# A two-layer hybrid attention trunk: another planned attention phase, and the first FFN weight splits pinned

## The chip, the core and the metric

The kernel runs on one core of one Trainium2 chip. The metric is the device time of one execution in microseconds (us), the median of several runs. TensorE (PE) multiplies, VectorE (DVE), ScalarE (ACT) and GpSimd (POOL) do the elementwise work, and SyncE (SP) issues most of the transfers.

## The reference

Two layers are computed on 512 tokens of width 1024. Each layer normalizes, projects to 3080 columns, runs four differential heads and eight forgetting heads, projects back, adds the residual, and runs a SwiGLU FFN of width 2816 between norms.

```python
for l in range(DEPTH):                       # DEPTH = 2
    proj = rms_norm(x, attn_pre_g[l]) @ w_in[l]
    qa, ka, va, qb, kb, vb, f_logit = split(proj)
    qa, ka = partial_rotary(qa, cos, sin), partial_rotary(ka, cos, sin)   # 16 of 64 columns of a head
    oa = rms_norm(diff_attention(qa, ka, va, lam), diff_sub_g[l]) * (1 - lam_init)   # softmax0 - lam * softmax1
    ob = forgetting_attention(qb, kb, vb, log_sigmoid(f_logit + forget_bias[l]))
    x = x + rms_norm(concat(oa, ob) @ w_out[l], attn_post_g[l])
    h = rms_norm(x, ffn_pre_g[l])
    x = x + rms_norm((silu(h @ w_gate[l]) * (h @ w_up[l])) @ w_down[l], ffn_post_g[l])
```

## The kernel before

**Arithmetic.** A float32 product is made from three matmuls in the reduced float format. Each operand is split into a high part (a cast on ScalarE, `hi`, names with h) and a low part (the difference on VectorE or GpSimd, `lo`, names with l); `hh`, `hl` and `lh` are summed in PSUM. So each weight chunk costs one DMA into a raw buffer (`wr`, two of them), one cast and one difference, and no matmul with the low part can run before the difference is done. Activations are kept transposed as `hT_h` and `hT_l`.

**The planned attention phase.** All instructions of a layer's attention are added to a `Plan` (L71) with an engine, an estimated duration, their dependencies, a key (lower is more urgent) and the buffers that they take and give. `Plan.run` (L98) simulates the engines, picks the most urgent ready operation of each, and issues it. Every issued instruction is passed to `keep_in_program_order`, which ties an instruction behind the one traced last on the same engine; so each engine executes the plan's order. The estimates are `dV`, `dA` and `dG` (L372 to L379) for VectorE, ScalarE and GpSimd. Softmax steps have keys by head and query block; the projections (`tile_chunk`, L670) and the output projection's first half (`o0_chunk`, L1090) are fillers with the key 1e6, run by TensorE whenever nothing more urgent is ready.

**The start of layer 0.** `start` (L397) loads `x` and the value weights, normalizes each of four token tiles, transposes them and computes the values `va` of the tiles, with the keys 500 and up, ahead of all fillers; warm-up matmuls on zeros (`WARM`, on `sinT`) fill TensorE's gaps. `tables` (L525) then computes the rotary tables: positions by eight DMAs on SP, the angles on VectorE, sine and cosine on ScalarE, out to DRAM and back into `cosT` and `sinT`. The rotation of k and q (`t1`, `pair`, `t2`, `t3` in `tile_chunk`) waits for them. Layer 1 has no such start: its norms and values come out of the end of the first FFN.

**The end of the phase.** After the plan, the last output matmuls run tile by tile. `o_norm(t)` is `post_norm` (L304) and then `pre_norm` (L279): squares on ScalarE, the reciprocal root on GpSimd, products on VectorE. `o_norm(3)` is at L1195. After it, L1263 asks for the first chunks of the FFN:

```python
(g0, g0_part), (u0, u0_part), (g1, g1_part) = gate(0), up(0), gate(f1)
g0_part(h0)                      # h0: tokens 0 to 255
pre_T(2, hs[2], f"f{l}", [0])    # transposes of token tile 2
```

`gate` and `up` call `proj_T` (L320), which calls `load_w` (L247): a DMA, a cast on ScalarE and a difference on VectorE. These are not pinned before the change; a list scheduler places them by its own estimate of when they are ready. The matmuls and transposes of this stretch are pinned (`pinned[0]` is true from L618 to L1281). The second up chunk, `up(f1)`, follows the first SwiGLU product (L1278). The other chunks of the FFN, from L1282 on, are not pinned.

Of the kernel before, what the change touches and what calls it, by code (L numbers as in the profile page):

```python
# [17 lines left out]
P = 128  # L18
# [17 lines left out]
TB = S // 16  # L36
VA_C, VA_T = 4, 1
# [7 lines left out]
C_ID, C_M, C_F, NKEEP, C_U = 0, 128, 640, 641, 641  # L45
# [16 lines left out]
class Op:  # L62
    def __init__(self, eng, dur, fn, deps, key, take, give, lat):
        self.eng, self.dur, self.fn, self.key, self.take, self.give, self.lat = eng, dur, fn, key, take, give, lat
        self.users, self.after, self.left, self.ready, self.end = [], [], 0, 0.0, None
        for d in deps:
            d.users.append(self)
            self.left += 1


class Plan:  # L71


    def __init__(self, slots, margin):
        self.free = {k: [0.0] * n for k, n in slots.items()}
        self.margin, self.ops, self.last, self.idle = margin, [], {}, None

    def add(self, eng, dur, fn, deps=(), key=0.0, take=(), give=(), lat=0.0, order="", ready=0.0):
        o = Op(eng, dur, fn, deps, key, take, give, lat)
# [18 lines left out]
    def run(self, pin, first):  # L98
        clock = dict.fromkeys("VAGQ", 0.0)
        clock["P"] = first  # L100
        cands = {e: [o for o in self.ops if o.eng == e and not o.left] for e in clock}
        todo = len(self.ops)
        while todo:
            best = None
            for e, c in cands.items():
                opts = []
                for o in c:
                    s = self.slots_at(o)
                    if s is not None:
                        r = max(s, o.ready)  # L110
                        opts.append((max(r, clock[e]), o.key, r, o))
# [12 lines left out]
            clock[o.eng] = start + o.dur  # L124
            o.end = start + o.dur + o.lat
# [34 lines left out]
def _constants():  # L160
# [6 lines left out]
    c[:, C_M + S - P:C_M + S] = np.where(r[None, :] > r[:, None], np.float32(-BIG), np.float32(0.0))  # L167
    expo = np.arange(0, ROT, 2, dtype=np.float32) / np.float32(ROT)
    inv_freq = (np.float32(1.0) / np.power(np.float32(500000.0), expo).astype(np.float32)).astype(np.float32)
    c[:, C_F] = inv_freq[r // 16]  # L170
    return c
# [3 lines left out]
def hymba_block(ctx, tc, x_d, pos_d, apre_d, win_d, fb_d, lq1_d, lk1_d, lq2_d, lk2_d, dsg_d, wout_d, apost_d,  # L175
# [64 lines left out]
    V.memset(sinT, 0.0)  # L240
    G.memset(cosT, 1.0)
# [5 lines left out]
    def load_w(src, shape, name, eng=None, dst=None, raw=None):  # L247
# [10 lines left out]
        A.copy(hi, raw)  # L258
        (eng or V).tensor_sub(lo, raw, hi.bitcast(F32))  # L259
# [87 lines left out]
    for l in range(DEPTH):  # L347
        win = win_d[l]
        with ExitStack() as actx:
# [12 lines left out]
            mixed_d = ap.tile([P, NDIFF, S], F32, name=f"mixd{l}", tag="v8", bufs=5)  # L362
            if l == 0:
                raw_v = ap.tile([P, NDIFF, S], F32, name=f"rawv{l}", tag="v8", bufs=5)
# [18 lines left out]
            vd, tab = [], []  # L383
# [12 lines left out]

            def start():  # L397

                plan.free.update(g=[], v8=[0.0], qs=[], ks=[])
# [9 lines left out]
                idd = dma(con[:, :P], con_d[:, :P], P)  # L409

                def w_load(c):
                    raw = (mixed_d, raw_v)[c // 2][:, 2 * (c % 2):2 * (c % 2) + 2]
                    if c == 0:
                        dst = q_tile("wva0h"), q_tile("wva0l")
                    elif c < 3:
                        w = k_tile(f"wva{c}")
                        dst = w[:, 0], w[:, 1]
                    else:
                        dst = [wpool.tile([P, WCH], F32R, name=f"{x}_va3", tag=x).rearrange("p (a b) -> p a b", a=2)
                               for x in ("wh", "wl")]  # L420
                    hi, lo = dst
# [1021 lines left out]
```

## Time and profile before

| what | us |
|---|---|
| median of three runs (1230.33 to 1235.37) | 1233.08 |
| the profiled execution | 1233.1 |
| its span, first to last instruction | 1231.3 |
| TensorE busy | 1195.3 |
| VectorE busy | 816.5 |
| ScalarE busy | 597.1 |
| GpSimd busy | 214.1 |

Layer 0 is planned attention from 0 to about 247, the seam to about 267.5, and its FFN to about 600; layer 1 follows in the same way, with its seam at 855 to 876. In a window table each engine has its busy time and, in brackets, the number of its instructions; PEclk is the granted share of TensorE's full clock of 2.4 GHz. A timeline row gives start and duration in us, the engine, the line, and the operation as out<-in; in square brackets stands the idle time ahead of it and what ended it. A matmul's row is longer than its share of TensorE, since the next one starts before its modelled end.

### The profile page before, as it was taken

What the parts mean: (1) busy time and instruction counts of PE and PEld (TensorE: products, weight loads), DVE (VectorE), ACT (ScalarE), POOL (GpSimd) and SP (SyncE); (2) the same over time, 40 slices, a digit from 0 to 9 for tenths busy, and PEclk for the clock granted to TensorE, in tenths of its full rate; (3) what the DMA queues carried; (4) which work ended last, traced back from release to release, by engine and by line L of the source; (5) the groups of instructions that cost most, each with busy time, mean ns of one, the idle gap of its engine ahead of it and who ended that gap; (6) DMA issues with size and microseconds to landing.
All of it is one profiled execution on the core that took longest, in us unless ns stands there. A gap on an engine that the chain in (4) does not pass through costs nothing.

```text
span 1231.3 us, 16721 instructions
## 1 busy us (share of the span) xinstructions
PE 1195.3 (97%) x5817; PEld 987.0 (80%) x5817; DVE 816.5 (66%) x1574; ACT 597.1 (48%) x1158; POOL 214.1 (17%) x250
## 2 busy tenths in 40 slices
PE   8998999999999999999999999999999999999997
PEld 5787877788888888888777878777988888888886
DVE  7698858765554555577848987695656455455776
ACT  5476657553332323365644767674533332333643
POOL 1302457320000000000223124672200000000010
PEclk9999999999999999999999999999999999999999
DMA  7333433416576676798513333433167667677964
GB/s 234 88 91 88 119 99 110 151 35 195 182 235 197 210 229 192 234 321 297 187 32 98 95 91 97 124 104 118 52 201 225 206 202 237 182 238 239 312 231 137
DMA packets 211268, 206.75 MB, mean 168 GB/s; under 512 B 11680, under 2 KB 155680, under 8 KB 211184
## 3 DMA queue, kind: packets, MB, share of 16 engines
q1 hardware_dynamic: 211040, 205.16, 53.5%
q8 instruction: 46, 0.75, 0.2%
q10 hardware_dynamic: 144, 0.52, 0.1%
q14 instruction: 38, 0.31, 0.1%
HBM read 163.34 MB, written 33.91 MB: 160 GB/s over the span
## 4 chain that ended last, share of the span: by engine, by line
PE 76%; DVE 11%; issue 7%; ACT 3%; POOL 2%; DMA 1%; POOLq 0%; DVEq 0%; SPq 0%; ACTq 0%
PE pj_g L205 20%; PE pj_u L205 19%; PE o L205 5%; PE da L205 5%; PE dc L205 5%; PE va L205 3%; PE pj_kd L205 3%; PE pj_kf L205 2%; PE db L205 2%; PE pj_qf L205 2%; PE vb L205 1%; DVE t2kd L739 1%; PE of L205 1%; PE pj_qd L205 1%; PE ptf L210 1%
## 5 line engine op out<-in xcount | busy, mean ns | idle before, releaser
L205 PE MATMUL pj_g<-hT_h,wh_g 128*128 128x512 f32 (+1 forms) x384 | 142.9, 372 | 0.0
L205 PE MATMUL pj_g<-hT_h,wl_g 128*128 128x512 f32 (+1 forms) x384 | 142.6, 371 | 0.0
L205 PE MATMUL pj_g<-hT_l,wh_g 128*128 128x512 f32 (+1 forms) x384 | 142.6, 371 | 0.0
L205 PE MATMUL pj_u<-hT_h,wh_u 128*128 128x512 f32 (+1 forms) x368 | 140.1, 381 | 0.0
L205 PE MATMUL pj_u<-hT_l,wh_u 128*128 128x512 f32 (+1 forms) x368 | 139.8, 380 | 0.0
L205 PE MATMUL pj_u<-hT_h,wl_u 128*128 128x512 f32 (+1 forms) x368 | 139.7, 380 | 0.0
L271 POOL TENSOR_SCALAR v_fp<-s_fp 128x1 f32<-128x1 f32 x8 | 7.6, 946 | 664.4 <-DVE c L1369 625.1
L259 DVE TENSOR_TENSOR wl_u<-wr_u,wh_u 128x1024 fp32r<-128x1024 f32 x44 | 53.9, 1225 | 99.6 <-ACT wh_u L258 99.6
L258 ACT CAST wh_g<-wr_g 128x1024 fp32r<-128x1024 f32 x44 | 46.4, 1054 | 146.3 <-PE pj_u L205 99.0
L258 ACT CAST wh_u<-wr_u 128x1024 fp32r<-128x1024 f32 x44 | 46.3, 1053 | 135.5 <-PE pj_g L205 128.3
L1239 DVE TENSOR_TENSOR sg<-pj_u,sg 128x512 f32<-128x512 f32 x44 | 30.4, 691 | 84.6 <-PE pj_u L205 84.6
L205 PE MATMUL da<-wh_d,op 128*128 128x512 f32 x264 | 82.6, 390 | 0.0
L205 PEld LDWEIGHTS pj_g<-hT_h,wh_g 128*128 128x128 f32 x384 | 72.3, 188 | 12.5
L205 PEld LDWEIGHTS pj_g<-hT_l,wh_g 128*128 128x128 f32 x384 | 72.3, 188 | 12.6
L205 PEld LDWEIGHTS pj_g<-hT_h,wl_g 128*128 128x128 f32 x384 | 72.3, 188 | 12.5
L205 PEld LDWEIGHTS pj_u<-hT_l,wh_u 128*128 128x128 f32 x368 | 69.2, 188 | 13.1
L205 PEld LDWEIGHTS pj_u<-hT_h,wl_u 128*128 128x128 f32 x368 | 69.2, 188 | 13.1
L205 PEld LDWEIGHTS pj_u<-hT_h,wh_u 128*128 128x128 f32 x368 | 69.2, 188 | 13.0
L258 ACT CAST wh_d<-wr_d 128x1024 fp32r<-128x1024 f32 x42 | 44.2, 1053 | 43.6 <-PE da L205 8.9
L259 DVE TENSOR_TENSOR wl_d<-wr_d,wh_d 128x1024 fp32r<-128x1024 f32 x42 | 51.3, 1221 | 17.7 <-ACT wh_d L258 17.5
L258 ACT CAST wh_d<-xr 128x1024 fp32r<-128x1024 f32 (+1 forms) x42 | 38.1, 908 | 43.7 <-PE da L205 13.2
L205 PEld LDWEIGHTS da<-wh_d,op 128*128 128x128 f32 x264 | 49.6, 188 | 10.2
(298 smaller groups left out, 3085.4 us busy)
## 6 DMA issues: line engine op xcount, KB each, us to landing
wr_g<-in_w_gate_dram SPq DMA_DIRECT2D x44, 512.0 KB, 4.6
wr_u<-in_w_up_dram SPq DMA_DIRECT2D x44, 512.0 KB, 4.6
b<-in_w_down_dram SPq DMA_DIRECT2D x88, 256.0 KB, 3.3
t_d<-b SPq DMA_DIRECT2D x88, 256.0 KB, 4.2
wr_d<-t_d SPq DMA_DIRECT2D x24, 512.0 KB, 4.6
wr_d<-in_w_down_dram SPq DMA_DIRECT2D x18, 512.0 KB, 5.0
wr_o<-in_w_out_dram SPq DMA_DIRECT2D x16, 512.0 KB, 4.4
xr<-t_d SPq DMA_DIRECT2D x16, 512.0 KB, 4.8
```

The lines of the kernel that those rows point to most:

```text
L205: ins = PE.matmul(out, a, b, start=start, stop=stop)
L210: ins = PE.transpose(out, a, idn)
L258: A.copy(hi, raw)
L259: (eng or V).tensor_sub(lo, raw, hi.bitcast(F32))
L271: G.tensor_scalar(v, s2[:, 0:1], scalar1=s2[:, 1:2], scalar2=EPS, op0=ALU.add, op1=ALU.add)
L739: return V.tensor_mul(b["t2"], b["t2"], sinT)
L1239: V.tensor_mul(sg, pu, sg)
```

## The change

There are three parts.

1. **The plan.** The estimates become longer (`dV` 110 + 1.05n, `dA` 115 + 0.83n, `dG` 180 + 2.17n, and some single ones). An operation can be marked with `port`; all of GpSimd's are, and those of VectorE that read and write SBUF alone. In the simulation a marked operation of one of the two engines waits until the other's marked one is over. The low parts of the first output-projection chunks move from GpSimd to VectorE.
2. **The start of layer 0.** The rotary tables are computed in `rotary`, from positions in a token-per-partition layout, with the key -95, ahead of the norms (-90 and up): one DMA on ScalarE's queue, about 27 small VectorE operations, eight sines on ScalarE, eight transposes on TensorE and two copies. The table set for the sine is loaded first. The value matmuls of token tiles 2 and 3 get a key just below the fillers', and the k and q projections of head 0 one that is lower by 20. The value weights lie in other buffers, so that the first k and q buffers are free.
3. **The pins.** `load_w` gets `pin`; `proj_T` passes `pinned[0]`. So the cast and the difference of gate 0, up 0, the second gate chunk and the second up chunk of each layer are tied behind the instruction traced last on their engine.

```diff
-VA_C, VA_T = 4, 1
+VA_C, VA_T, VA_EARLY = 4, 1, 2
...
+                        if o.port:
+                            r = max(r, port["G" if e == "V" else "V"])
...
+            if o.port:
+                port[o.eng] = start + o.dur
...
-    def load_w(src, shape, name, eng=None, dst=None, raw=None):
+    def load_w(src, shape, name, eng=None, dst=None, raw=None, pin=False):
...
         nc.sync.dma_start(raw, src)
-        A.copy(hi, raw)
-        (eng or V).tensor_sub(lo, raw, hi.bitcast(F32))
+        for ins in (A.copy(hi, raw), (eng or V).tensor_sub(lo, raw, hi.bitcast(F32))):
+            if pin:
+                tc.keep_in_program_order(ins)
         return hi, lo
...
-        wh, wl = load_w(src_w[:, col:col + P].rearrange("(k p) n -> p k n", p=P), [P, KT, P], name)
+        wh, wl = load_w(src_w[:, col:col + P].rearrange("(k p) n -> p k n", p=P), [P, KT, P], name, pin=pinned[0])
...
             def dV(n):
-                return 68 + 1.04 * n
+                return 110 + 1.05 * n
 
             def dA(n):
-                return 60 + 0.83 * n
+                return 115 + 0.83 * n
 
             def dG(n):
-                return 120 + 2.15 * n
+                return 180 + 2.17 * n
...
+                tc.keep_in_program_order(A.preload_act_table_set("trig_and_small"))
...
+                rotary()
...
-                                         key=500 + VA_C * c + VA_T * t)
+                                         key=(500 if t < VA_EARLY else FILLER - 20) + VA_C * c + VA_T * t)
...
+            def rotary():
+                key = -95
...
+                v = op("A", 500, lambda: A.dma_start(pos, pos_d[0].rearrange("(j p) -> p j", p=P)), [], lat=3000)
+                v = op("V", 80, lambda: V.tensor_copy(pf, pos), [v])
+                v = op("V", 700, lambda: [lambda f=f, c=c: V.tensor_scalar_mul(an[:, f * NT:(f + 1) * NT], pf, c)
+                                          for f, c in enumerate(_inv_freq())], [v])
                 for sc in (2.0 ** 22, 2.0 ** 11, 1.0):
...
+                for z, dep in ((0, v2), (1, v)):
+                    a = op("A", 800, lambda z=z: [place(z, half, m) for half in range(2) for m in range(2)], [dep])
+
+                    def tr(z=z):
+                        x[z] = (bank_t, bank_s)[z](f"rot{z}")
+                        for j in range(NT):
+                            transpose(x[z][:, j * P:(j + 1) * P], tabs[z][:, j * P:(j + 1) * P], ident)
+                    p = op("P", 436, tr, [a, idd[0]], take=["ts"[z]])
+                    ends.append(op("A", dA(S), lambda z=z: A.copy((cosT, sinT)[z], x[z]), [p], give=["ts"[z]]))
+                add("A", 0, lambda: None, ends, key=-99, give=["rc", "rc", "rd"])
...
             def tables(last):
...
+                du = add("Q", 1.43 * S, sums, key=1, lat=2000, order="ld rc", take=["rc"])
...
                 return box, add("G" if eng is G else "V", dG(n) if eng is G else dV(n), lo, [a], key=URGENT,
-                                give=["wr"])
+                                give=["wr"], port=True)
...
+                last_tile[:] = fillers([(650, piece(k)) for k in range(KT)], [ready], take={0: ["g"]}, give=["w"],
+                                       key=FILLER - 40 if kind == "d" and l == z == 0 else FILLER)
...
-                v3 = add("V", dV(S), t2, [v2], key=key)
-                g1 = add("V", dV(S), t3, [v3], key=key, give=["rd"])
+                v3 = add("V", dV(S), t2, [v2], key=key, port=True)
+                g1 = add("V", dV(S), t3, [v3], key=key, give=["rd"], port=True)
...
-                v = add("V", dV(n), top, [o], key=n_key, give=["s"])
-                return b, add("A", 282 + 0.83 * n, expo, [v], key=n_key)
+                v = add("V", dV(n)+80, top, [o], key=n_key, give=["s"])
+                return b, add("A", 370 + 0.87 * n, expo, [v], key=n_key)
...
                 box, ready = load(wout_d[l][kc * P:(kc + 2) * P, :S].rearrange("(k p) n -> p k n", p=P), [P, 2, S],
-                                  f"o0{l}{kc}")
+                                  f"o0{l}{kc}", eng=V)
```

## Rows read from the trace of the kernel before

**Rows 1.** The head of the page: the span, and each engine's busy time.
```profile
span 1231.3 us, 16721 instructions
PE 1195.3 (97%) x5817; PEld 987.0 (80%) x5817; DVE 816.5 (66%) x1574; ACT 597.1 (48%) x1158; POOL 214.1 (17%) x250
```
**Rows 2.** Window table: from:to, length, engines' busy us (instructions), PEclk, DMA share, GB/s.
```profile
0.00:12.20 12.20, 8.41 (x27) 3.87 (x27) 4.99 (x9) 5.45 (x12) 1.69 (x10) 0.88 0.82 300
...
38.40:120.00 81.60, 76.92 (x416) 63.81 (x415) 69.81 (x176) 52.36 (x122) 19.19 (x8) 1.00 0.32 85
120.00:190.00 70.00, 68.64 (x384) 57.26 (x383) 49.23 (x143) 46.05 (x111) 33.07 (x43) 1.00 0.41 114
190.00:247.00 57.00, 52.97 (x270) 41.74 (x269) 45.28 (x109) 35.84 (x83) 32.46 (x38) 1.00 0.41 130
...
267.50:600.00 332.50, 332.26 (x1542) 277.99 (x1540) 198.71 (x283) 129.65 (x193) 8.93 (x10) 1.00 0.69 224
...
644.60:730.00 85.40, 80.32 (x427) 66.32 (x428) 73.04 (x182) 54.07 (x124) 19.20 (x8) 1.00 0.36 96
730.00:800.00 70.00, 68.38 (x389) 57.28 (x388) 49.98 (x149) 45.99 (x114) 35.85 (x49) 1.00 0.40 111
800.00:855.00 55.00, 50.48 (x250) 40.37 (x249) 42.75 (x97) 34.22 (x77) 29.70 (x32) 0.97 0.40 125
```
**Rows 3.** Timeline of PE, last value matmul and first k projection of layer 0.
```profile
38.22 0.39 PE L205 MATMUL va<-wh_va,hT_l 128*128 128x512 f32 x1
38.44 0.39 PE L205 MATMUL pj_kd<-hT_h,wh_kd 128*128 128x512 f32 x1
```
**Rows 4.** Timeline of ACT, PE and DVE around the seam of layer 0.
```profile
234.07 1.05 ACT L258 CAST wh_g<-wr_g 128x1024 fp32r<-128x1024 f32 x1
...
267.47 0.28 PE L205 MATMUL pj_g<-hT_h,wh_g 128*128 128x256 f32 x1
...
272.23 0.63 ACT L277 ACTIVATE junk<-xs 128x512 f32<-128x512 f32 x1
...
275.30 0.74 DVE L286 SCALAR_TENSOR_TENSOR h_f<-xs,r_f,g_fpre 128x512 f32<-128x512 f32 x1
...
284.82 1.23 DVE L259 TENSOR_TENSOR wl_g<-wr_g,wh_g 128x1024 fp32r<-128x1024 f32 x1 [0.20 <-ACT wh_g L258]
```
**Rows 5.** Timeline of PE and DVE at the seam of layer 1.
```profile
876.12 0.28 PE L205 MATMUL pj_g<-hT_h,wh_g 128*128 128x256 f32 x1
...
883.83 0.74 DVE L286 SCALAR_TENSOR_TENSOR h_f<-xs,r_f,g_fpre 128x512 f32<-128x512 f32 x1
```
**Rows 6.** Timeline of POOL and DVE from 45: a weight split and a rotation step.
```profile
45.03 2.39 POOL L649 TENSOR_TENSOR wl_qd<-wr_qd,wh_qd 128x1024 fp32r<-128x1024 f32 x1 [2.82 <-ACT wh_qd L645]
45.47 2.50 DVE L739 TENSOR_TENSOR t2kd<-t2kd,sinT 128x512 f32<-128x512 f32 x1
```
**Rows 7.** Line L739, that step in both layers: duration ns min/median/max.
```profile
L739 DVE TENSOR_TENSOR t2kd<-t2kd,sinT x8: 686/2056/2505, 45.5 to 721.3; 128x512 f32<-128x512 f32 x8
```
**Rows 8.** Timeline of PE at the first scores.
```profile
56.28 0.41 PE L205 MATMUL sd<-ksd,qsd 128*128 128x128 f32 x2 [0.68 <-issue]
```
**Rows 9.** Timeline of DVE, a part of the rotary tables.
```profile
28.34 0.65 DVE L563 SCALAR_TENSOR_TENSOR rot<-rot 128x32 f32<-128x32 f32 x3
```
**Rows 10.** Window table of the first 50 us, as rows 2.
```profile
10.00:20.00 10.00, 9.97 (x48) 6.91 (x46) 8.40 (x14) 9.49 (x24) 3.93 (x6) 0.87 0.78 275
20.00:30.00 10.00, 9.99 (x48) 8.24 (x48) 9.66 (x24) 4.67 (x6) 0.00 (x0) 1.00 0.58 144
...
40.00:50.00 10.00, 10.00 (x45) 8.26 (x44) 5.85 (x7) 2.52 (x4) 4.61 (x2) 1.00 0.33 82
```
**Rows 11.** Timeline of PE, transposes of the second token tile.
```profile
14.42 1.14 PE L210 MATMUL hp_a<-con,h_a 128*128 128x128 f32 x8
```
**Rows 12.** The page's DMA issues: KB each, us from issue to landing.
```profile
wr_g<-in_w_gate_dram SPq DMA_DIRECT2D x44, 512.0 KB, 4.6
```
**Rows 13.** Timeline of PE near the end of layer 1's attention.
```profile
837.53 0.30 PE L210 MATMUL ptf<-con,ae 128*128 128x128 f32 x1 [1.96 <-DVE ae L1037]
```
**Rows 14.** Window table just behind it, as rows 2.
```profile
838.60:842.00 3.40, 3.40 (x11) 2.62 (x10) 2.60 (x9) 2.69 (x7) 0.00 (x0) 0.50 0.54 153
```

More of the change, by code (lines that the diff above doesn't have):

```diff
@@ L62, with __init__ @@
 class Op:
-    def __init__(self, eng, dur, fn, deps, key, take, give, lat):
+    def __init__(self, eng, dur, fn, deps, key, take, give, lat, port):
         self.eng, self.dur, self.fn, self.key, self.take, self.give, self.lat = eng, dur, fn, key, take, give, lat
+        self.port = port or eng == "G"
         self.users, self.after, self.left, self.ready, self.end = [], [], 0, 0.0, None
@@ L76, in __init__, with add @@
         self.margin, self.ops, self.last, self.idle = margin, [], {}, None
-    def add(self, eng, dur, fn, deps=(), key=0.0, take=(), give=(), lat=0.0, order="", ready=0.0):
-        o = Op(eng, dur, fn, deps, key, take, give, lat)
+    def add(self, eng, dur, fn, deps=(), key=0.0, take=(), give=(), lat=0.0, order="", ready=0.0, port=False):
+        o = Op(eng, dur, fn, deps, key, take, give, lat, port)
         o.ready = ready
@@ L100, in run @@
         clock["P"] = first
+        port = {"V": 0.0, "G": 0.0}
         cands = {e: [o for o in self.ops if o.eng == e and not o.left] for e in clock}
@@ L426, in w_load @@
                         a = add("A", dA(S), lambda k=k: A.copy(hi[:, k], raw[:, k]), [d], key=-85 + c,
-                                take=["w"] if c == 3 and k == 0 else [], order="hi w" if c == 3 and k == 0 else "")
+                                take=["w"] if c == 2 and k == 0 else [], order="hi w" if c == 2 and k == 0 else "")
                         ops += [a, add("V", dV(S) + 80, lambda k=k: V.tensor_sub(
@@ L515, in start @@
                         done[t, c] = add("P", 1390, vas, hT[t, c // 2] + wl[c] + ([done[t, c - 1]] if c else []),
-                                         key=500 + VA_C * c + VA_T * t)
+                                         key=(500 if t < VA_EARLY else FILLER - 20) + VA_C * c + VA_T * t)
                     vd_split(t, [done[t, 3]])
-                for c in range(4):
-                    add("P", 0, lambda: None, [done[t, c] for t in range(NT)], key=-99,
-                        give=(["qs", "qs"], ["ks"], ["ks"], ["w"])[c])
@@ L521, in start, with mix @@
-                add("P", 0, lambda: None, wl[2] + wl[3], key=-99, give=["v8"])
+                def mix():
+                    nonlocal mixed_d
+                    mixed_d = ap.tile([P, NDIFF, S], F32, name=f"mixd{l}", tag="v8", bufs=5)
+                add("P", 0, lambda: None, sum(wl.values(), []), key=-99, give=["pt", "pt"])
+                half, full = ([done[t, c] for t in range(NT)] for c in (1, 3))
+                add("P", 0, lambda: None, half, key=-99, give=["v8", "v8"])
+                add("P", 0, lambda: None, full, key=-99, give=["v8", "w"])
@@ L547, in sums @@
                 def sums():
                     x["tu"] = rbuf("rc", F32, "tu")
-                    return x["tu"]
-                dp = add("Q", 3000, positions, key=1, lat=2000, order="ld rd", take=["rd"])
-                dc = get(lambda: con[:, P:], con_d[:, P:NKEEP], S)
-                du = get(sums, con_d[:, C_U:C_U + S], S, take=["rc"])
-                v = op("V", 100, lambda: V.tensor_copy(x["a"], x["p"]), [dp])
-                v = op("V", 100, lambda: V.tensor_scalar_mul(x["a"], x["a"], con[:, C_F:C_F + 1]), [v, dc])
@@ L687, in piece @@
                     return fn
-                last_tile[:] = fillers([(650, piece(k)) for k in range(KT)], [ready], take={0: ["g"]}, give=["w"])
+                last_tile[:] = fillers([(650, piece(k)) for k in range(KT)], [ready], take={0: ["g"]}, give=["w"],
+                                       key=FILLER - 40 if kind == "d" and l == z == 0 else FILLER)
                 done = last_tile[-1]
@@ L719, in stack @@
                         d = dV(S) if eng == "V" else dG(S)
-                        e = add(eng, d, lo(m), [a], key=key, give=give if m else [])
+                        e = add(eng, d, lo(m), [a], key=key, give=give if m else [], port=kind == "d")
                         if which == "k":
@@ L1002, in diff_head @@
                     mixed_d[:, h], mixed_d[:, h], dsg[:, l:l + 1], b["nrm"], op0=ALU.mult, op1=ALU.mult), [a, c],
-                    key=key + LAG_SS, give=["e"])]
+                    key=key + LAG_SS, give=["e"], port=True)]
             def fox_head(hh, n0):
```

134 lines of the change are left out of this document (66 added, 68 removed).

## The prediction

> **What bounds the kernel now.** I read the head of the page first. TensorE is busy in 97% of a span of 1231.3 us [rows 1], so nothing can be gained but its idle time, and everything that makes it wait is paid in full. The windows by stage say where that idle time lies [rows 2]. From 267.5 to 600, in the FFN of layer 0, it is 332.50 - 332.26 = 0.2 us. In the planned attention of layer 0 it is 4.7 + 1.4 + 4.0 = 10.1 us (three rows from 38.4 to 247), in that of layer 1 it is 5.1 + 1.6 + 4.5 = 11.2 us (three rows from 644.6 to 855), and 12.2 - 8.4 = 3.8 us lie in the start. These rows understate a stall: a 128x512 matmul is shown for 0.39 us while the next one begins 0.23 us later [rows 3], so about 0.16 us of each stall hides under the last matmul. With some twenty stalls of that kind a layer I count 10 to 14 us of stalls in each attention phase that a better order could remove. In the same windows VectorE is busy for 69.8 of 81.6 us and 73.0 of 85.4 us: it is what TensorE waits for. The other place that matters is the seam between attention and FFN, where TensorE now passes from the last output-projection matmul to the first gate matmul without a pause, at 267.47 and at 876.12 [rows 4, 5].
>
> **The plan (both layers).** VectorE loses time to GpSimd. `t2kd` runs 2.50 us from 45.47 while a 2.39 us weight split holds GpSimd from 45.03; the same form takes 0.686 us alone and 2.056 us in the median of its eight runs [rows 6, 7]. The old planner does not know this and counts 600 ns for a 512-column VectorE operation. The new one counts 648 ns, keeps the two engines' operations on that port apart, and gives the first output chunks' splits to VectorE. VectorE pays for that with four splits of 1.23 us a layer and GpSimd saves four of about 2.4 us [rows 4, 6]. Lower bound of the effect: a TensorE loss of 5 us a layer, as much as one window row's idle time once more, since an order that keeps engines apart can also make a bias row or a transpose late and nothing in this trace shows the new order. Upper bound: a gain of all 14 us. The visible idle time shrinks, I take it, to somewhat under half, because the rest are dependent steps of a head with no filler beside them, as at 56.28, where TensorE stood 0.68 us before the first scores [rows 8]. I take a gain of 8 us in each layer, nearer to the middle than to either end.
>
> On that port a rule of the Trainium skill is worth weighing. "SBUF — State Buffer", section "SBUF: two separate sides", calls the shared pair an exclusive lock that whoever starts first holds for the whole instruction, with a VectorE operation of two SBUF inputs locked out only by a GpSimd operation that reads SBUF. The 2.50 us row agrees: `t2kd` ended 0.55 us after the split did. By the rule GpSimd is locked out just as well, so part of what the plan takes from VectorE would come back as late bias rows; by it alone the gain would be 5 us a layer and the sum 6 us higher.
>
> **The start of layer 0.** The tables move from the stretch 26 to 33 to the first microseconds, with a higher key than the norms. That is about 27 small VectorE operations, 0.65 us for a group of three [rows 9], some 5.5 us of VectorE. It is busy 8.4 of 10 us from 10 to 20 and 9.7 of 10 us from 20 to 30 [rows 10]. Some 3 us of the chain can lie in its idle time ahead of 8 us; the rest delays norms and splits, and with them the first value matmuls. Bounds: 0 if the positions land before 4 us, 5.5 us if the whole chain comes ahead of the norms; I take 2.5 us. The eight table transposes on TensorE are priced by the nearest row, eight in 1.14 us [rows 11]: 1.1 us, and twice that at most, at half the clock. The positions' DMA and the table load go onto ScalarE's queue ahead of its first square, which waits for `x` anyway; I cost them at nothing, and if that cover is gone they delay the first norm by their own length. On SP the eight position loads go away. The load of the prefix sums now takes a buffer that the tables hold, and the first k and q weights queue behind it, so these weights may land no sooner than now.
>
> **The first head early.** The k projection of head 0 starts at 38.44 [rows 3] because all four value tiles are ahead of it. With only two ahead, and behind the last transposed tokens, it can start at 28 to 34. The matmuls are the same, so this pays only in stalls: VectorE has 4.2 us free of 10 between 40 and 50 [rows 10] and is the limit after 55. I have put that into the 8 us of layer 0, whose upper end it raises by 4.
>
> **The pinned splits (both layers).** Now the splits of gate 0 and up 0 float forward: `wh_g` runs at 234.07, within attention [rows 4]. A pinned split stands behind whatever its engine was given last before it. In program order that is neither the planned phase nor its end but `o_norm(3)` at L1195: on ScalarE the second square of `pre_norm(3)`, on VectorE the second norm product of `pre_norm(3)`. Both come after the last output tile, since they need `o1[3]`. TensorE's next work, `g0_part(h0)`, needs only tokens 0 to 255 but needs `wh_g` and `wl_g`, and TensorE's own order is pinned as well, so nothing else can run there.
>
> Layer 0, from the rows as they are: last output matmul, then 267.47. The second square of token tile 3 begins at 272.23 and ends at 272.86, and with the read of its accumulator ScalarE is free at about 272.95; `wh_g` (1.05) then ends at 274.0. The second norm product begins at 275.30 behind an `hT_l` split of 0.68 that will no longer be due then, so it ends at about 275.4; `wl_g` (1.23) ends at 276.65 [rows 4]. With 0.15 to be seen, the third matmul starts at 276.8. Two 256-column matmuls run at 274, 0.24 us together. The stall is 276.8 - 267.5 - 0.2 = 9.1 us. Layer 1 in the same way: 876.12, second norm product at 883.83 less 0.6, so `wl_g` at 885.2 and a stall of 9.0 us [rows 5].
>
> What is late next: the raw buffer of the second gate chunk comes free only when `wl_g` is done, its load takes 4.6 us [rows 12], cast and difference 1.05 and 1.23, so it is ready at 276.65 + 6.9 = 283.5; TensorE, with 46 matmuls of 0.12 (half of 0.23) and eight transposes of 1.14 before it [rows 11], wants it at 283.5 too. The second up chunk stands behind the first Silu and its products. For both I take 0.8 us a layer, bounds 0 and 2.5.
>
> Last the clock. After 1.96 us of idle time at 837.53 the granted clock was 0.50 from 838.6 to 842.0 [rows 13, 14], the 1.2 GHz level, and in those 3.4 us TensorE did the work of 1.7. After a stall of 9 us I take one such stretch, 1.7 us a layer, bounds 0 and 3.4. So the pins cost 9.05 + 0.8 + 1.7 = 11.5 us a layer, 23 us in all (17 to 30). What they give back: `wh_g` and `wl_g` leave the end of attention, 2.3 us of engines that are not late there; it is inside the 8 us.
>
> **Sum.** The profiled execution took 1233.1 us, its span plus 1.8, and equals the median of 1233.08. 1233.1 - 8 - 8 + 2.5 + 1.1 + 23 = 1243.7; I say 1244 us.
>
> **The rivals.**
> The pins do not bind (place: the seam of both layers; price: 23 us). If the splits still run before 267, because the edge ties them to an earlier instruction than I read, the sum is 1233.1 - 16 + 3.6 = 1220.7 us, faster. It decides from the point where `wl_g` ends before the last output matmul. For it: the tie goes to one instruction of the same engine, and no row here shows a tie of this kind at work. Against: the code of `o_norm(3)` stands between the planned phase and `gate(0)`, and issues on both engines. Chance 0.2.
> The plan gains nearly all that is idle, 14 us in layer 1 and 16 in layer 0 with the early head: 1233.1 - 30 + 3.6 + 23 = 1229.7, or 1235.7 with 12 a layer, no change. For it: 2.056 against 0.686 us [rows 7]. Against: the 0.68 us at 56.28 [rows 8], and others of its kind, wait for a chain and not for a busy engine. Chance 0.15.
> The plan gains nothing: GpSimd's bias rows wait for VectorE, the scores for them, and what VectorE wins is lost there (place: the fox heads; price: the 16 us). It decides once the bias row of a score ends behind that score's turn on TensorE: 1233.1 + 3.6 + 23 = 1259.7, slower, or 1256 if a quarter of the gain stays. For it: VectorE is busy for 86% of the window from 38.4 to 120 already [rows 2]. Against: GpSimd is given four splits a layer less. The rule of the lock weighed above points this way, and no row here goes that far. Chance 0.13.
> My case has the remaining 0.52, with 1235 to 1252.
>
> **Chances.** What a measurement here can tell from no change is 0.5%, 6.2 us, so slower begins at 1239.3 and faster at 1226.9. My case: 0.40 slower, 0.12 same. Pins without effect: 0.17 faster, 0.03 same. Strong plan: 0.12 same, 0.03 faster. Weak plan: 0.13 slower. Together 0.20 faster, 0.27 same, 0.53 slower. The range leaves out the outer part of the first and the last rival: 1218 to 1257 us.
>
> **What would show it.** Pins: `wh_g` and `wl_g` of each layer's first gate chunk behind the squares and norms of tile 3, a gap on TensorE of about 9 us ahead of the first `pj_g` and a clock of 0.5 after it. If `wh_g` still stands within attention, the second step is wrong and the time is near 1220. Plan: `t2kd` at about 0.7 us, and idle time of TensorE in the three windows a layer down from 10 and 11 us to 4 or 5. Start: first `pj_kd` before 34, first `va` not later than 15. The forecast fails most easily by the size of the plan's gain, which no row of this trace shows.

## The result and the profile after

The changed kernel takes 1240.07 us in the median (1238.91 to 1241.09), against 1234.54 us before. The ratio on record is 1.0051, 95% interval 1.0038 to 1.0064 (the two medians alone give 1.0045). It is slower, by about the half per cent that can just be told from no change. The forecast was 1244 us, with 1218 to 1257 as its range. In what follows each kernel is compared with the kernel before by its ratio; 1% is 12.3 us.

The head of the page of after, which answers to [rows 1]:
```profile
span 1238.4 us, 16740 instructions
...
PE 1195.7 (97%) x5826; PEld 995.1 (80%) x5826; DVE 808.5 (65%) x1588; ACT 598.5 (48%) x1164; POOL 198.1 (16%) x243
```
TensorE's work is the same but for the eight transposes of the tables (0.9 us at 0.11 each), so nearly all of the 7.1 us are waiting or half clock. The window table of after by stage, to be read beside [rows 2] (the first window begins at the first `pj_kd` of after):
```profile
31.90:120.00 88.10, 87.19 (x468) 74.08 (x468) 73.05 (x185) 54.51 (x123) 21.01 (x11) 1.00 0.40 105
120.00:190.00 70.00, 70.00 (x410) 60.72 (x409) 50.75 (x152) 50.16 (x123) 34.90 (x50) 1.00 0.38 106
190.00:247.00 57.00, 55.89 (x280) 44.52 (x279) 42.62 (x105) 33.63 (x82) 25.82 (x30) 1.00 0.32 97
...
261.28:271.52 10.24, 6.67 (x29) 6.37 (x30) 3.69 (x4) 2.58 (x4) 0.86 (x2) 0.50 0.62 197
...
644.60:730.00 85.40, 77.95 (x407) 65.41 (x408) 68.47 (x176) 50.51 (x120) 19.55 (x8) 0.96 0.34 90
730.00:800.00 70.00, 70.00 (x407) 61.05 (x406) 51.16 (x152) 49.27 (x117) 35.78 (x50) 1.00 0.44 125
800.00:855.00 55.00, 52.48 (x268) 41.96 (x267) 41.78 (x107) 33.74 (x81) 22.09 (x27) 1.00 0.33 101
```
TensorE's idle time in the attention of layer 0 is down from 10.1 to 0.91 + 0 + 1.11 = 2.0 us. In layer 1 it is 7.45 + 0 + 2.52 = 10.0 us against 11.2. The window at 261.28 is new: 10.24 us at a granted clock of 0.50. The early head and the rotation step in after, one group of line L768 (against [rows 7]) and two lines of PE's timeline (against [rows 3]):
```profile
L768 DVE TENSOR_TENSOR t2kd<-t2kd,sinT x8: 674/688/2502, 39.0 to 725.6; 128x512 f32<-128x512 f32 x8
```
```profile
31.71 0.39 PE L214 MATMUL va<-wvh,hT_l 128*128 128x512 f32 x1
31.94 0.39 PE L214 MATMUL pj_kd<-hT_h,wh_kd 128*128 128x512 f32 x1
```
The step takes 0.688 us in the median instead of 2.056, with two of the eight still at 2.5, and the first k projection begins 6.5 us sooner.

The seam of layer 0 in the timeline of after (PE, ACT, DVE), against [rows 4]:
```profile
256.41 0.40 PE L214 MATMUL o<-wo1h,hT_l 128*128 128x512 f32 x1
...
261.25 0.63 ACT L286 ACTIVATE junk<-xs 128x512 f32<-128x512 f32 x1
...
261.88 1.03 ACT L266 CAST wh_g<-wr_g 128x1024 fp32r<-128x1024 f32 x1
...
262.96 0.58 PE L214 MATMUL pj_g<-hT_h,wh_g 128*128 128x256 f32 x1 [6.16 <-ACT wh_g L266]
263.05 1.42 DVE L295 SCALAR_TENSOR_TENSOR h_f<-xs,r_f,g_fpre 128x512 f32<-128x512 f32 x2 [1.98 <-POOL r_f L281]
264.38 1.22 DVE L266 TENSOR_TENSOR wl_g<-wr_g,wh_g 128x1024 fp32r<-128x1024 f32 x1
...
265.65 0.58 PE L214 MATMUL pj_g<-hT_h,wl_g 128*128 128x256 f32 x1 [1.89 <-DVE wl_g L266]
```
The cast stands behind the second square of token tile 3 and the difference behind the second norm product of that tile; TensorE, with nothing else in its order, waits for both. Layer 1 shows the same at 879.26 (6.18) and 881.95 (1.89), against [rows 5].

To see small stalls too, I sum over the trace what passes from the start of one matmul to the start of the next beyond the spacing of the same shape undisturbed (0.23 us for 512 columns, 0.12 for 256, 0.11 for a transpose). It holds stalls and half clock together, in us:

| Kernel | 0 to 40 | attention 0 (40 to 240) | seam 0 (to 300) | to 640 | attention 1 (to 860) | seam 1 (to 920) | rest | sum |
|---|---|---|---|---|---|---|---|---|
| before | 7.2 | 18.9 | 0.2 | 4.0 | 22.2 | 0.2 | 0.4 | 53.2 |
| after | 7.8 | 6.7 | 12.0 | 4.0 | 18.7 | 11.1 | 0.1 | 60.2 |
| e1, no pin | 7.6 | 9.3 | 0.5 | 5.8 | 25.0 | 0.2 | 0.1 | 48.5 |
| e2, before with pins | 7.3 | 18.0 | 12.4 | 2.8 | 19.3 | 11.3 | 0.1 | 71.2 |
| e3, early pins | 7.4 | 6.4 | 0.2 | 4.9 | 16.5 | 0.0 | 0.7 | 36.2 |
| e7, late head | 7.4 | 17.5 | 0.8 | 5.4 | 18.9 | 0.2 | 0.1 | 50.4 |
| e8, no port rule | 7.9 | 25.5 | 0.7 | 3.8 | 24.2 | 0.3 | 0.6 | 63.0 |
| e9, before with early pins | 7.8 | 22.3 | 0.4 | 3.9 | 20.9 | 0.3 | 0.5 | 56.0 |

So the change gains 12.2 us in attention 0 and 3.5 in attention 1, and pays 11.8 and 10.9 us at the two seams. Differences of 2 us in one column say little: after and e3 have the same plan and the same longest stall in attention 1 (3.46 us), but the half clock behind it lasted 6.8 us in after and 3.4 in e3, and the columns have 18.7 and 16.5.

The largest single loss of layer 1 lies at one place, in the timeline of after (DVE, POOL, PE):
```profile
705.30 0.16 DVE L979 TENSOR_TENSOR ld<-ld,nlam 128x1 f32<-128x1 f32 x1
...
705.61 2.35 POOL L678 TENSOR_TENSOR wl_kf<-wr_kf,wh_kf 128x1024 fp32r<-128x1024 f32 x1 [1.64 <-ACT wh_kf L674]
...
706.14 0.16 DVE L978 RECIPROCAL ld<-ld 128x2 f32<-128x2 f32 x1
706.34 1.64 DVE L979 TENSOR_TENSOR ld<-ld,nlam 128x1 f32<-128x1 f32 x1
...
709.50 0.77 PE L214 MATMUL pj_kd<-hT_h,wh_kd 128*128 128x512 f32 x1 [3.30 <-DVE vf L824]
```
The same product of one element a partition takes 0.16 us, and 1.64 us when a GpSimd split is running: it ends when the split ends. The new planner leaves this operation out of its rule for the port. It is not the only one: the small operations behind the forget logits and the `hT_l` splits that `conv` gives to VectorE also read and write SBUF alone, and are added without `port`. Behind the product in VectorE's queue stands `vf`, which has to empty the bank that `pj_kd` waits for. Within the stall the granted clock falls to 0.50, from 708.4 to 715.25. Stall and half clock are 6.3 us by the sum of the table, about half of the 12.0 us by which attention 1 loses more than attention 0.

### The profile page after: what moved, and what is told of

It is laid out like the page before. It is cut to its first block, busy times and chain, and to the rows that moved or that the text cites. A ratio compares the mean times of both kernels' runs of the same rounds, so it can differ in the third digit from the quotient of the medians.

```text
span 1238.4 us, 16740 instructions
## 1 busy us (share of the span) xinstructions
PE 1195.7 (97%) x5826; PEld 995.1 (80%) x5826; DVE 808.5 (65%) x1588; ACT 598.5 (48%) x1164; POOL 198.1 (16%) x243
## 4 chain that ended last, share of the span: by engine, by line
PE 84%; issue 6%; DVE 5%; POOL 2%; ACT 1%; DMA 0%; POOLq 0%; DVEq 0%; SPq 0%; ACTq 0%
PE pj_g L214 20%; PE pj_u L214 19%; PE da L214 5%; PE dc L214 5%; PE pj_kd L214 4%; PE vb L214 4%; PE pj_kf L214 4%; PE pj_qd L214 4%; PE pj_qf L214 3%; PE o L214 3%; PE va L214 3%; PE db L214 2%; PE sd L214 1%; PE sf L214 1%; PE of L214 1%
## 5 line engine op out<-in xcount | busy, mean ns | idle before, releaser
L214 PE MATMUL pj_g<-hT_h,wh_g 128*128 128x512 f32 (+1 forms) x384 | 145.4, 379 | 12.3 <-ACT wh_g L266 12.3
L214 PEld LDWEIGHTS pj_g<-hT_l,wh_g 128*128 128x128 f32 x384 | 74.4, 194 | 12.4
L266 DVE TENSOR_TENSOR wl_g<-wr_g,wh_g 128x1024 fp32r<-128x1024 f32 x44 | 53.7, 1221 | 13.8 <-ACT wh_g L266 12.2
L266 DVE TENSOR_TENSOR wl_d<-wr_d,wh_d 128x1024 fp32r<-128x1024 f32 x42 | 51.3, 1221 | 17.5 <-ACT wh_d L266 15.4
```

Source lines behind the costliest of these rows:

```text
L214: ins = PE.matmul(out, a, b, start=start, stop=stop)
L266: for ins in (A.copy(hi, raw), (eng or V).tensor_sub(lo, raw, hi.bitcast(F32))):
```

## The experiments

**The pins.** e1 takes them off, e2 puts them alone on the kernel before, e3 keeps them and moves what they stand behind.

e1:
```diff
-        wh, wl = load_w(src_w[:, col:col + P].rearrange("(k p) n -> p k n", p=P), [P, KT, P], name, pin=pinned[0])
+        wh, wl = load_w(src_w[:, col:col + P].rearrange("(k p) n -> p k n", p=P), [P, KT, P], name)
```


> The changed kernel with the weight splits of all gate and up chunks left unpinned, as in the kernel before; all else as changed. Theory: the pins cost about 11.5 us in layer 0 and 10.9 in layer 1 (stall of TensorE ahead of the first pj_g and half clock after it) and the planned phase keeps its gain, so 1240.1 - 22.4 = 1217.7 us, 0.986 of the kernel before, with pj_g of both layers behind the last output matmul without a gap and no stretch of half clock there. Rival: the stall only moves (a split that floats forward into the planned phase takes VectorE and GpSimd time from the last heads), so that half or more of it comes back there: 1229 us or above.

Measured: 1228.37 us, ratio 0.9964 (0.9950 to 0.9978). The seams are free, as the theory has it, but the gain is 0.87% or 10.7 us and not 22: the rival holds in its size. The tail of attention 1 in the timeline of e1 (ACT, DVE, PE):
```profile
832.11 1.05 ACT L266 CAST wh_g<-wr_g 128x1024 fp32r<-128x1024 f32 x1 [3.57 <-DMA wr_g<-in_w_gate_dram]
833.06 0.72 ACT L915 ACTIVATE ae<-ae,mf 128x512 f32<-128x512 f32 x1
...
833.99 1.21 DVE L266 TENSOR_TENSOR wl_g<-wr_g,wh_g 128x1024 fp32r<-128x1024 f32 x1
...
836.27 1.23 DVE L266 TENSOR_TENSOR wl_u<-wr_u,wh_u 128x1024 fp32r<-128x1024 f32 x1
836.29 1.11 PE L219 MATMUL ptf<-con,ae 128*128 128x128 f32 x4 [3.69 <-DVE mixf L1093]
```
A floating cast took a place in ScalarE's queue ahead of the last head's exponential and waited 3.57 us there for its load; `wl_g` and `wl_u` then stood in VectorE's queue among that head's steps. TensorE lost 3.7 us at that point. By the table the attention phases of e1 lose 2.6 and 6.3 us more than those of after. So a pin behind the plan gives back 8.9 us a run of the 22.7 that it takes.

e2: the lines of the diff in `load_w` and `proj_T` on the kernel before, nothing else.

> The kernel before with only the pin added to the splits of the gate and up chunks that are requested while the order is pinned. Theory: the price belongs to the pin and not to the new plan, so the same two stalls appear here: 1234.5 + 22.4 = 1257 us, ratio 1.018. Rival: in the old order the seam has other work to offer (its tail ends elsewhere), and the pin costs less than half: 1246 us or below. By the pin's own worth as a way to keep the tail of attention clear it would even gain: below 1234.

Measured: 1254.0 us, ratio 1.0169 (1.0144 to 1.0194), 20.8 us above the kernel before, near the 22.4 expected. The seam of layer 0 in the timeline of e2 (PE):
```profile
273.43 0.58 PE L205 MATMUL pj_g<-hT_h,wh_g 128*128 128x256 f32 x1 [6.60 <-ACT wh_g L258]
...
276.12 0.58 PE L205 MATMUL pj_g<-hT_h,wl_g 128*128 128x256 f32 x1 [1.90 <-DVE wl_g L258]
```
The same two waits as in after, so they belong to the pin and not to the plan. From e2 to the changed kernel the plan and the start gain 1.0169 - 1.0051 = 1.18%, 14.5 us.

e3 (`got` goes to the `proj_T` of gate 0 and up 0; all other gate and up splits are unpinned):
```diff
             plan.run(tc.keep_in_program_order, first)
+            got = {"g": first_w(wg_d[l], 0, f"g{l}0", True), "u": first_w(wu_d[l], 0, f"u{l}0", True)}
```


> The changed kernel with the splits of gate 0 and up 0 still pinned, but requested directly behind the planned phase, ahead of the norms of the four output tiles; the second gate and up chunk are unpinned. Theory: not the pin but what it stands behind (the last norm of token tile 3) costs the 8.5 us a layer: here the splits run before the output tiles end, the gap ahead of pj_g is gone, and the time is within 4 us of the run without pins: 1217 to 1222 us. Rival: a pinned split costs wherever it stands, since on VectorE and ScalarE it now holds up the norms of the output tiles, which feed the transposes that TensorE has in between: 1228 us or above, with stalls ahead of hp_f.

Measured: 1216.07 us, ratio 0.9859 (0.9836 to 0.9881): better than either expected, and below both kernels. The seam of layer 0 in the timeline of e3 (ACT, DVE, PE):
```profile
235.03 1.04 ACT L266 CAST wh_g<-wr_g 128x1024 fp32r<-128x1024 f32 x1
...
237.24 1.22 DVE L266 TENSOR_TENSOR wl_u<-wr_u,wh_u 128x1024 fp32r<-128x1024 f32 x1
...
255.74 0.39 PE L214 MATMUL o<-wo1h,hT_l 128*128 128x512 f32 x1
255.97 0.28 PE L214 MATMUL pj_g<-hT_h,wh_g 128*128 128x256 f32 x1
```
The splits lie behind the last planned operation and some 18 us ahead of their first use, so neither the tail nor the seam waits. Against e1 it is 1.05% less, 12.9 us; the table gives 2.9 us of that to attention 0 and 8.5 to attention 1. Two things differ from e1, the pin and the earlier place of the request. An early request without the pin was not run, so it is not shown which of the two keeps the tail clear here.

e9 asks whether the early pin is worth that by itself: the edit of e3 on the kernel before.

> The kernel before (old plan, old tables, late head) with the splits of gate 0 and up 0 requested and pinned directly behind its planned phase, ahead of the norms of the output tiles, and no other pin. Theory: an early pin keeps the last heads of the old plan clear too, but there the floating splits lie in a tail that is not as tight; the profile with the late pins shows some 3 us less loss there than the kernel before: 1229 to 1231 us. Rival: the floating splits cost the old plan what they cost the new one (1228.4 - 1216.1 = 12.3 us): 1220 to 1222 us.

Measured: 1235.22 us, ratio 1.0016 (1.0002 to 1.0031). Neither was right: the old plan gains nothing. Its tail stall is its own, in the timeline of e9 (POOL, DVE, PE):
```profile
839.20 2.35 POOL L653 TENSOR_TENSOR wo1l<-wr_o,wo1h 128x1024 fp32r<-128x1024 f32 x1
...
839.41 2.23 DVE L1041 TENSOR_SCALAR ae<-ae,lf 128x128 f32<-128x128 f32 x1
...
841.78 0.30 PE L210 MATMUL ptf<-con,ae 128*128 128x128 f32 x1 [1.87 <-DVE ae L1041]
```
A scaling of 128 columns took as long as the split beside it, and the transposes waited. The kernel before has this stall at 837.53 [rows 13]. Layer 0 of e9 has it too (1.88 us at 233.27), and there the table's loss rises from 18.9 to 22.3 us, more than layer 1 gains. In the old plan a clear tail brought nothing, since this stall does not come from the floating splits.

**The half clock.** e5 fills the seam with matmuls that nothing keeps.
```diff
+            for _ in range(68):
+                mm(g0[:, h0], hT_h[:, 0, :P], hT_h[:, 0, h0], True, True)
             g0_part(h0)
```


> The changed kernel, pins and all, with 68 matmuls of 256 columns ahead of the first gate matmul of each layer; they write the bank that the first gate matmul starts anew, so they fill the gap of TensorE (6.33 + 2.19 us in layer 0, 6.35 + 2.19 in layer 1) and change nothing that is kept. Theory: the gap costs twice, once as the wait of 8.5 us and once by the granted clock of 0.5 behind it (about 2.9 and 2.0 us); with TensorE busy through the wait the second part alone goes: 1240.1 - 4.9 = 1235 us, with the first pj_g after the filling at the same place relative to wl_g and the clock at 1.0 after it. Rival: the half clock costs nothing on its own, because the next splits are late anyway: 1239 to 1241 us.

Measured: 1239.3 us, ratio 1.0046 (1.0030 to 1.0061), against 1.0051: no difference that can be told, and not the 4.9 us of the theory; the time lies in the rival's range. Layer 0 of e5, timeline (PE) and window table:
```profile
256.37 8.32 PE L214 MATMUL pj_g<-hT_h 128*128 128x256 f32 x68
...
265.37 0.39 PE L214 MATMUL pj_g<-hT_h,wl_g 128*128 128x256 f32 x1 [0.45 <-DVE wl_g L266]
...
272.80 0.38 PE L214 MATMUL pj_g<-hT_h,wl_g 128*128 128x256 f32 x1 [0.55 <-DVE wl_g L266]
```
```profile
264.60:285.00 20.40, 19.41 (x161) 18.99 (x160) 7.24 (x10) 6.93 (x10) 0.00 (x0) 1.00 0.36 104
```
The clock is 1.00 where after had 0.50, but the second gate chunk is then wanted sooner than its raw buffer, load and split allow, and TensorE waits for that instead (0.55 us here, 0.57 and 0.76 in layer 1). In layer 1 this takes the place of the half clock in full: from the first matmul with `wl_g` to the first SwiGLU step (`sg` on ScalarE) it is 15.13 us, against 15.06 in after. In layer 0 it does so in part, 14.10 against 15.90: there 1.8 us of the 2.9 come back, less than the two medians can tell apart.

**The parts of the plan,** each taken out of e3.

e7:
```diff
-VA_C, VA_T, VA_EARLY = 4, 1, 2
+VA_C, VA_T, VA_EARLY = 4, 1, 4
...
-                                       key=FILLER - 40 if kind == "d" and l == z == 0 else FILLER)
+                                       key=FILLER)
```


> The kernel with the early pins (1216.1 us), with all four value tiles ahead of the first head's k and q projection again, as in the kernel before; tables, durations and port as changed. Theory: the gain of layer 0's attention over that of layer 1 (about 12 against 4 us) comes largely from the early head: 4 to 7 us more here, 1220 to 1223 us, all of it between 30 and 110 us of the span. Rival: the gain is that of the measured durations and the port, and the early head is worth nothing: 1215 to 1217.

Measured: 1229.35 us, ratio 0.9965 (0.9951 to 0.9979): 1.06% or 13 us lost, about twice what was expected. In the table attention 0 goes back from 6.4 to 17.5 us, near to the 18.9 of the kernel before. Timeline of e7 (POOL, DVE, PE):
```profile
101.61 2.35 POOL L681 TENSOR_TENSOR wl_kf<-wr_kf,wh_kf 128x1024 fp32r<-128x1024 f32 x1 [1.63 <-ACT wh_kf L677]
...
102.35 1.63 DVE L982 TENSOR_TENSOR ld<-ld,nlam 128x1 f32<-128x1 f32 x1
...
105.51 0.76 PE L214 MATMUL pj_kd<-hT_h,wh_kd 128*128 128x512 f32 x1 [3.29 <-DVE vf L827]
```
Without the early head layer 0 has, to 0.01 us, the blocked product and the stall that layer 1 has at 706.34 and 709.50 in after. Layer 1 has no early head in any of these kernels; giving it one was not tried.

e8:
```diff
-                        if o.port:
-                            r = max(r, port["G" if e == "V" else "V"])
```


> The kernel with the early pins (1216.1 us), with the planner's rule for the shared port taken away: VectorE and GpSimd operations may be planned side by side; measured durations, tables and early head as changed. Theory: the port rule carries most of the plan's gain in both layers; without it 512-column VectorE operations of 2 us come back beside GpSimd's splits, and 6 to 12 us are lost: 1222 to 1228 us. Rival: the measured durations and the move of the output chunks' splits to VectorE carry it: within 3 us of 1216.

Measured: 1241.75 us, ratio 1.0055 (1.0037 to 1.0074): 1.96% or 24 us lost, more than expected, and worse than the old plan. Timeline of e8 (POOL, DVE):
```profile
105.89 2.37 POOL L679 TENSOR_TENSOR wl_kf<-wr_kf,wh_kf 128x1024 fp32r<-128x1024 f32 x1 [8.27 <-ACT wh_kf L675]
106.44 1.83 DVE L980 TENSOR_TENSOR ld<-ld,nlam 128x1 f32<-128x1 f32 x1
```
Such meetings are back in both layers, and `t2kd` has a median of 1.233 us where after has 0.688.

e11 puts back `dV`, `dA` and `dG`, the lengths by which the planner counts:
```diff
-                return 110 + 1.05 * n
+                return 68 + 1.04 * n
```


> The kernel with the early pins (1216.1 us), with the planner's three length formulas for VectorE, ScalarE and GpSimd as in the kernel before (600 instead of 648 ns for 512 columns on VectorE); port rule, tables, early head as changed. Theory: without the rule 25.7 us were lost, so the rule carries the plan and the measured lengths only sharpen it: 2 to 6 us lost, 1218 to 1222 us. Rival: a rule that keeps two engines apart works only with true lengths, and 10 us or more are lost: 1226 us or above. Below 1216 if the lengths were no gain.

Measured: 1223.52 us, ratio 0.9923 (0.9903 to 0.9942): 0.64% or 8 us lost, a little over the expected.

e12:
```diff
-                              f"o0{l}{kc}", eng=V)
+                              f"o0{l}{kc}")
```


> The kernel with the early pins (1216.1 us), with the splits of the first output chunks back on GpSimd, as in the kernel before. Theory: with the port rule a split of 2.4 us on GpSimd shuts VectorE out of the port for that long, while on VectorE it takes 1.23: four of them a layer, in the stretch of the fox heads where VectorE is busy for 73 of 100 us; 3 to 8 us lost, 1219 to 1224 us, between 190 and 235 us and between 790 and 835 us of the span. Rival: VectorE has room there, and the place of these splits is worth nothing: within 2 us of 1216.

Measured: 1228.91 us, ratio 0.9960 (0.9945 to 0.9976): 1.01% or 12 us lost, more than expected. Timeline of e12 (POOL, DVE, PE):
```profile
204.84 2.75 POOL L681 TENSOR_TENSOR wo1l<-wr_o,wo1h 128x1024 fp32r<-128x1024 f32 x1 [0.24 <-ACT wo1h L677]
...
205.28 2.86 DVE L1104 TENSOR_TENSOR hT_l<-mixf,hT_h 128x512 fp32r<-128x512 f32 x1
...
209.23 2.78 POOL L681 TENSOR_TENSOR wl_o<-wr_o,wh_o 128x1024 fp32r<-128x1024 f32 x1
...
209.74 3.45 DVE L1070 TENSOR_SCALAR ae<-ae,lf 128x512 f32<-128x512 f32 x3
...
212.45 1.30 PE L219 MATMUL ptf<-con,ae 128*128 128x128 f32 x5 [5.92 <-DVE ae L1070]
```
An `hT_l` split (2.86 us, where the one at 209.14, begun ahead of its neighbour on GpSimd, took 0.68) and then the first of three scalings meet splits on GpSimd, one after the other, and TensorE waits 5.92 us, although the planner's rule stood. The first meeting it does not cover, since `conv` adds the `hT_l` split without the mark. The scaling is marked and met a split all the same, as two `t2kd` in after did: the rule keeps apart what meets in the planner's own times, and the chip's times differ from them. What these four parts are worth adds up to 57 us, where the whole of plan and start, from e9 to e3, is worth 1.57% or 19 us: the parts do not add. A likely reason, not tested, is that the planner lays out everything anew without each one.

**The stall of layer 1.** e4 (on e1), e6 and e10 (on e3) try to remove it.
```diff
-                    v = add("V", 250, rl, [x[0][1], x[1][1]], key=key)
+                    v = add("V", 250, rl, [x[0][1], x[1][1]], key=key, port=True)
```


> As the run without pins, and the planner is told that the small operations on the sums of the differential heads (the reciprocal and the product with the one-element column of lambda) need the port shared with GpSimd, which the change leaves unmarked. Theory: the 3.46 us stall of TensorE at 709.5 in layer 1, behind a one-element product that took 1.64 us beside a GpSimd weight split, goes away with the half clock after it: 4 to 6 us below the run without pins, 1212 to 1214 us. Rival: the stall came from a full VectorE queue at that place and not from the port, or a later start for these small operations makes the heads late elsewhere: within 2 us of the run without pins, or above it.

Measured: 1224.16 us, ratio 0.9928 (0.9903 to 0.9952). The time is 0.36% below e1, but not for the reason given. Timeline of e4 (POOL, DVE, PE):
```profile
700.26 2.36 POOL L678 TENSOR_TENSOR wl_kf<-wr_kf,wh_kf 128x1024 fp32r<-128x1024 f32 x1 [1.63 <-DVE lg L811]
...
700.80 1.87 DVE L843 SCALAR_TENSOR_TENSOR az<-lg 128x32 f32<-128x32 f32 x1
...
704.09 0.76 PE L214 MATMUL pj_kd<-hT_h,wh_kd 128*128 128x512 f32 x1 [3.23 <-DVE vf L824]
```
The product is clear of the split, the next unmarked operation of 32 columns is not, and the stall stays. By the trace the gain came in the tail of layer 1, where in the new order the floating cast waited 1.13 us for its load (827.88) in place of the 3.57 of e1.

e6 marks that one too, on top of e3:
```diff
-                    deps = [add(eng, 110, fn, deps, key=key)]
+                    deps = [add(eng, 110, fn, deps, key=key, port=eng == "V")]
```


> The kernel with the early pins (1216.1 us), and the planner told of the shared port for the small operations on sums of the differential heads and for the chain of eleven small operations behind the forget logits (az, u, ln, lg), all of 32 columns or fewer. In the run without pins and with the heads' operations alone marked, the wait only moved: the 32-column az took 1.87 us in place of 0.18 at the same place, and TensorE's stall stayed at 3.4 us. Theory: with both marked, no small operation of VectorE lies beside the split wl_kf there, the stall goes and the half clock after it too: 4 to 5 us less, 1211 to 1212 us. Rival: the next operation in the queue meets the split instead, or VectorE is simply short of time there: within 2 us of 1216, with the stall of 3 us still ahead of pj_kd near 697.

Measured: 1216.44 us, ratio 0.9849 (0.9829 to 0.9869), the same as e3. The product with lambda now takes 0.46 us at most and `az` 0.19, and layer 1 is better (12.9 us lost in place of 16.5), but layer 0 has a stall that e3 has not (10.5 in place of 6.4). Timeline of e6 (DVE, PE):
```profile
98.52 1.42 DVE L827 TENSOR_TENSOR vf<-vb,vf 128x256 fp32r<-128x256 f32 x4 [1.23 <-ACT vf L823]
...
99.09 0.47 PE L214 MATMUL pj_kd<-hT_h,wh_kd 128*128 128x512 f32 x1 [2.85 <-DVE vf L827]
```
Here VectorE itself waits for ScalarE's half of `vf`. So the blocked product was one cause of the stall; in layer 1 of e6 it is down from 3.46 to 1.93 us. The handing on of the value chunks' banks is another, and it is enough alone.

e10 projects the second value chunks of layer 1 after the fourth differential head:
```diff
-            for item in FILL.split():
+            for item in (FILL if l == 0 else "d0 d1 d2 d3 v1 f0 v0 f1 f2 f3").split():
```


> The kernel with the early pins (1216.1 us), with the second value chunks of layer 1 projected behind the fourth differential head's k and q and not ahead of it. Theory: the 3.46 us stall ahead of pj_kd in layer 1 is that of a bank of PSUM, held by the value chunks until VectorE has made vf, at the time when the weight split wl_kf holds GpSimd; in another order the two do not meet, and the stall and the half clock behind it go: 1211 to 1213 us. Rival: VectorE is short in that stretch whatever the order is, and the wait appears at the next projection: 1215 us or above.

Measured: 1217.11 us, ratio 0.9867 (0.9846 to 0.9888), the same as e3. The stall of 3.46 us is gone, and four of 1.4 to 1.9 us stand between 689 and 716 instead. The rival holds: the wait moves.

## Why the prediction was right

**The pins bind.** Right, with mechanism, place and price. `wh_g` came behind the second square of tile 3, `wl_g` behind its second norm product. The stall was put at 9.1 and 9.0 us; it is 8.5 in both layers (6.33 + 2.19 and 6.35 + 2.19 by spacing). For the late second chunk and the clock together 2.5 us were put; they are 12.0 - 0.2 - 8.5 = 3.3 and 11.1 - 0.2 - 8.5 = 2.4. The step that adds these two as separate costs was wrong, as e5 shows: without the half clock the wait takes its place, in layer 1 in full and in layer 0 in part. The half clock lasted 10.24 us a layer, where one stretch of 3.4 was taken. The 23 us stand against 22.7 by the table and 20.8 by e2; of the range of 17 to 30 the lower end is 18 by the prediction's own terms. The rival by which the pins do not bind is out.

**What the pins give back.** The prediction put it at nothing beyond the plan's 8 us, on the ground that ScalarE and VectorE are not late in the tail. That is the term that failed: with the new plan, unpinned splits lose 8.9 us in the two attention phases, 6.3 of them in layer 1 behind a cast that waits for its load. It did not spoil the sum, because the 16 us for the plan were taken with the pins in place. It does spoil the rival without effective pins, put at 1220.7 us: e1 without the pins is 10.7 us better than the change, not 23, and took 1228.37.

**The plan.** 8 and 8 us were put; the table gives 12.2 and 3.5, in sum 15.7. That this sum agrees is luck. The early head, folded into layer 0's 8 us as up to 4 more, is worth 13 us when it is taken out of e3 (e7). Without it the plan and the tables are 0.51% or 6.3 us better than the old plan with the same pins (e9), and not 16. So the plan without the early head was put too high and the early head too low, and the two errors cancelled. `t2kd` is at 0.688 us in the median, as forecast, against 2.056 [rows 7]. Layer 1 missed the forecast idle time of 4 to 5 us (10.0), in part through operations of 1 and 32 columns that the planner's rule leaves out and through the banks of the value chunks; e7 has the same stall in layer 0 when the early head is gone. Layer 0 passed the forecast (2.0).

**The rule weighed.** The Trainium skill, "SBUF — State Buffer", section "SBUF: two separate sides", has the lock held for the whole instruction and working both ways. These runs agree on both. A VectorE operation of 0.16 us took 1.64. On the other side a GpSimd split that began just behind a VectorE one took 3.38 us, in the timeline of after (DVE, POOL):
```profile
832.37 1.31 DVE L678 TENSOR_TENSOR wo1l<-wr_o,wo1h 128x1024 fp32r<-128x1024 f32 x1
832.58 3.38 POOL L678 TENSOR_TENSOR wo1l<-wr_o,wo1h 128x1024 fp32r<-128x1024 f32 x1
```
It ended 2.28 us after VectorE's did, and `wl_kf`, a split of the same size, takes 2.41 us in the median of eight. The loss that this would have brought to the sum, 6 us, had no row behind it and was not to be seen in the total: the sum without it is the nearer one.

**The start.** 2.5 us and 1.1 for the transposes were put. The first 40 us lose 0.6 us more than before, and eight transposes at the spacing of 0.11 are 0.9: together 1.5. The chain is spread over VectorE from 7.0 to 21.5 us of the span. First `pj_kd` at 31.94 (before 34 was forecast) and first `va` at 12.59 (not later than 15).

**The sum with the measured terms:** 1233.1 - 12.2 - 3.5 + 0.6 + 0.9 + 22.7 = 1241.6, against 1240.07. Of the rivals, a plan that gains nearly all held for layer 0 and one that gains little for layer 1, and they evened out.

## What to carry to other kernels

A pinned instruction waits for whatever its queue was given last, so ask where in the program its request stands: here the first splits, pinned, cost 22 us behind the last norm and nothing at the end of the plan, with the first use 18 us later. An instruction that floats is no safer, since in an in-order queue it can wait for its own load ahead of work that is ready. And a planner's rule for a shared resource has to cover every operation that touches it, the smallest too, and even then it holds only as far as the planned times do; when one is left out, or one is added, look for the next in the queue before you count the gain.

## What the runs showed of the hardware

How long a VectorE operation is held beside a GpSimd split did not depend on its size: one column took 1.64 us, 32 columns 1.87, 128 columns 2.23, and each ended about when the split did. The operation held need not have two tensors as inputs: `ae`, a scaling by one value a partition, was held for 2.23 us in e9. Not every one is held: the reciprocal of two columns at 706.14 in after took 0.16 us beside the split. Within the seam's gap of 6.33 us (layer 0 of after) the granted clock fell to 0.50 and stayed there for 10.24 us, against 3.40 us behind the gap of 1.96 us in the kernel before [rows 13, 14]. Taking it away won 1.8 us in layer 0 of e5 and nothing in layer 1, where the next weights were late anyway.
